# A two-layer encoder trunk on one core: page stores on other queues, one group in raw tiles, and row scaling spread over three products

## The chip, the core and the metric

The kernel runs on one core of a Trainium2 chip. A core has TensorE (PE in the profile) for matmuls, VectorE (DVE), ScalarE (ACT), GpSimd (POOL) and SyncE (SP), and 16 DMA engines that move data between HBM and the on-chip memory. Each engine works through its own list of instructions in order; semaphores tie the lists together. SP, ACT and POOL can issue DMAs; an engine whose next instruction is a DMA that may not start yet waits there, and all that follows in its list waits too. The metric is the device time of one execution in microseconds (us), as a median of several.

## The reference, cut to what matters

Two layers, each with a mixer and a SwiGLU feed-forward block, each followed by a layer norm over the residual sum. Layer 0 mixes by latent attention plus a two-dimensional Fourier transform, layer 1 by a gated unit with a 128 x 128 mixing of positions.

```python
def even_mixer(x, ...):
    h = x @ w_in
    c_q, c_kv, k_r, f = jnp.split(h, ...)
    q = (rms_norm(c_q, q_norm) @ w_uq)...   # nope part, rotary part
    k_nope, v = (c_kv @ w_uk)..., (c_kv @ w_uv)...
    attn = mla_attention(q_nope, q_rope, k_nope, k_rope, v)
    return jnp.concatenate([attn, fourier_mix(f)], axis=-1) @ w_out

def odd_mixer(x, ...):
    u, v = jnp.split(gelu(x @ w_in), 2, axis=-1)
    s = (einsum('gpq,bnqgc->bnpgc', w_s, layer_norm(v)) + b_s)
    return (u * s) @ w_out

for layer in range(2):
    y = even_mixer(x) if layer == 0 else odd_mixer(x)
    x = layer_norm(ALPHA * x + y, mix_ln_g[layer], mix_ln_b[layer])
    x = layer_norm(ALPHA * x + swiglu(x), ffn_ln_g[layer], ffn_ln_b[layer])
```

There are 1024 positions of width 1024, 8 heads, a feed-forward width of 2816, all in float32.

## The kernel before

**Numbers.** A float32 product is made of three matmuls. `split` (L133) turns an operand into a high part (ACT copies it into the matmul's rounded type, L135) and a low part (DVE subtracts, L136); `mm3` (L138) runs high x high (L141), high x low (L142) and low x high (L143). So each operand that comes from memory passes ACT, then DVE, then PE.

**Stages.** In the order of time: `even_front` (projection, norms, Fourier part) to about 150 us, `attention` to 560, the output product of the even mixer to 670, the first feed-forward block to 1330, the gated unit's front to 1680, its output product to 1840, and the second feed-forward block to the end. Between stages, data goes through pages in HBM: `mix0` to `mix11` hold the columns of the even mixer (0 to 7 the heads' outputs, 8 to 11 the Fourier groups), `tp` those of the odd mixer, `h` those of the feed-forward blocks.

**`reduce`** (L409) is the product that ends a mixer or a feed-forward block, together with the residual sum and the layer norm. It computes a 2 x 2 block product with seven products p = 1 to 7 in place of eight, which needs sums of blocks: SA, SB of the left pages, TA, TB of the weights. The sums are made ahead by `job` (L330: POOL loads two pages, DVE adds them at L317 to L320, POOL stores them). A product runs over M pairs of pages (M is 6 for the even mixer, "mix", 8 for the odd one, "odd", and 11 for the feed-forward blocks), taken two pairs at a time in n groups (3, 4 and 6). The products come in the order 1, 5, 6, 4, 7, 2, 3. Per group `load` (L440) has SP fetch the two operand tiles, one for the left side and one for the right (L396), and splits them into one of three pairs of cells (`xoh`, `xol`); PE then runs 4 position tiles x 2 pairs x 3 = 24 matmuls. The fetched tiles are called `rx`; there are six of them, placed where the stage before had its tiles. For the first two groups of "mix" `lead` (L405) fetches into raw weight tiles (`raw`, handed out in turn by `raw_tile`, L151) while attention still runs.

PE accumulates in eight banks: p = 1 uses four, p = 5 the other four; p = 6 goes on in those of p = 1, and p = 4 takes those of p = 5 over. So the sums of p = 1 must be added to the rows (`add`, L455, on DVE) before p = 6 starts, and those of p = 5 before p = 4 starts.

**Rows.** The residual rows are eight tiles, four of half 0 (`xt[0, s]`) and four of half 1. `residual` (L461) clears a word of the tile on DVE (L465), to order the tile's reuse, and POOL fetches the row block, 512 KB (L466). Except in "mix", `gained` (L468) multiplies it by the scale of the preceding layer norm and adds its bias (L472 and L473, 1024 wide, on DVE). The first `add` to a tile multiplies it by ALPHA as well (L458).

**Queues.** In the first layer SP issues, besides the weight loads (L158) and the swaps of the rotary part (L1103 and L1287), the stores of finished pages: 20 stores of the Fourier part (L1238, L1242, L1243) and 32 stores of attention's pages (L1360), each behind the ACT copy of the page (L1358). Each store waits on SP until its page is computed. The order of each engine's list is settled when the program is built; `behind` (L306) keeps an instruction behind a named one.

Of the kernel before, what the change touches and what calls it, by code (L numbers as in the profile page):

```python
# [112 lines left out]
class Trunk:  # L113
# [295 lines left out]
    def reduce(self, st, resid, rgb, ln, keep, pre=None, left=()):  # L409


        nc, a = self.nc, self.a
        lo, hi = self.LO, self.HI
        left = list(left)
        M = len(st["W"]) // 2
        groups = self.groups(st)
# [23 lines left out]
        def load(p, g):  # L440
            if (p, g) not in ops:
                with self.behind(*((self.last_a, self.last_v) if p == 1 and self.last_a is not None else ())):
                    ops[p, g] = self.stream(st, p, groups[g], raws, pairs)

        def mm(p, g, s):
            if p in (6, 7):
# [76 lines left out]


        def spread(jobs, k, of):
            i0, i1 = len(jobs) * k // of, len(jobs) * (k + 1) // of
            for j in jobs[i0:i1]:
                j()
        slots = range(4)
        for p in (1, 5, 6, 4, 7, 2):  # L530
            for g in range(n):
                load(p, g)
                if p == 1 and g == 1:
                    load(1, 2)
                    if rgb is not None:
                        rg, rb = (self.bcast(tmp(), a["ln_" + x][rgb[0], rgb[1]]) for x in "gb")
                    last = self.job(st, M - 1, True) if st is self.stage["mix"] else None
                if p == 1 and 0 < g < 3:
                    for s in (2 * g - 2, 2 * g - 1):
                        residual(0, s)  # L540
                if (p == 1 and g == n - 1) or (p == 5 and g == 0):
                    for s in (0, 1) if p == 1 else (2, 3):
                        residual(1, s)
                if p == 6 and g == 0 and keep is None:
                    fg, fb = (self.bcast(self.raw_tile(), a["ln_" + x][ln[0], ln[1]]) for x in "gb")
                if p == 4 and g == 0 and pre is not None:
                    with self.behind(*self.marks):
                        pre()
                if p == 1 and g > 1:
                    spread([lambda s=s: gained(0, s) for s in slots], g - 2, n - 1)  # L550
                if p == 5 and g == 0:
                    spread([lambda s=s: gained(0, s) for s in slots], n - 2, n - 1)
                if p == 5 and g > 0:
                    spread([lambda s=s: gained(1, s) for s in slots], g - 1, n - 1)
                if (p, g) == (5, 1):
                    for s in slots:
                        add(0, s, lo, 1, True)
                if p == 2:
                    spread([lambda s=s: normed1(s) for s in slots], g, n)
                for s in slots:  # L560
                    mm(p, g, s)
                    if p == 1 and s % 2 == 1 and left:
                        left.pop(0)()
                    if g == n - 1:
                        if p == 5:
                            add(0, s, hi, p, True)
                            add(1, s, hi, p, True)
                        elif p == 6:
                            add(0, s, hi, p)
                        elif p == 4:  # L570
                            add(1, s, lo, p, True, ALU.subtract)
                        elif p == 7:
                            add(1, s, lo, p)
                            add(1, s, hi, p)
                        elif p == 2:
                            add(0, s, lo, p)
                            stat(0, s, 0)
                if (p, g) == (5, 0) and last is not None:
                    last(self.marks[2])
# [566 lines left out]
    def fourier(self, fe, fo, f512, chan, mix):  # L1146
# [4 lines left out]
        with ExitStack() as es:  # L1151
# [75 lines left out]
            for i in range(2):  # L1227
                for j in range(2):
# [6 lines left out]
                    y, yv = y.rearrange("p (b h c) -> p b h c", b=2, h=2), ym.rearrange("p (b h c) -> p b h c", b=2, h=2)  # L1235
                    if j == 0:
                        for b in range(2):
                            nc.sync.dma_start(page[:, b], y[:, b])  # L1238
                    else:
                        for x in range(2):  # L1240
                            for b in range(2):
                                nc.sync.dma_start(page[x * H + 1:(x + 1) * H, b], y[x * H + 1:(x + 1) * H, b])  # L1242
                                nc.sync.dma_start(page[x * H:x * H + 1, b], yv[2 * i + x:2 * i + x + 1, b])  # L1243

    def attention(self, cq, ckv, kr, rc, rs, mix):
        nc, a = self.nc, self.a
        with ExitStack() as es:
# [102 lines left out]
            def pv(hp, h, qb):  # L1350
                d = st[hp]
                page, pt = T([P, 256], F32, "page"), d.pop(("ptr", h, qb))
                ps = self.mm_bank((P, 256))
                vh, vl = d["v"][h]
                for kt in range(NT):
                    ph, pl = (t[:, kt % 4, :] for t in pt[kt // 4])
                    self.mm3(ps, (vh[:, kt, :], vl[:, kt, :]), (ph, pl), kt == 0, kt == NT - 1)
                nc.scalar.copy(page, ps)  # L1358
                o = qb % 2 * 512 + qb // 2 * 256
                nc.sync.dma_start(mix[hp * 2 + h][:, o:o + 256], page)  # L1360

            def front(hp):
                qks = [lambda tb=tb, w=w: qk(hp, 0, w, tb) for w in "qk" for tb in range(2)]
# [54 lines left out]
```

## Time and profile before

| quantity | us |
|---|---|
| median of 3 runs (2510.45 to 2514.87) | 2513.96 |
| profiled execution, its own time | 2514.32 |
| its span, first to last instruction | 2512.5 |
| PE busy and idle in 150 to 560 (attention) | 401.58, 8.42 |
| PE busy and idle in 560 to 670 ("mix" reduce) | 102.69, 7.31 |
| PE busy and idle in 1185 to 1330 (ffn reduce, first) | 144.06, 0.94 |
| PE busy and idle in 1680 to 1840 ("odd" reduce) | 145.13, 14.87 |
| PE busy and idle in 2275 to 2512.5 (ffn reduce, last) | 218.44, 19.06 |

The stretches come from the view that sums each engine's busy time by windows. A row of the timeline reads: start, duration, engine, line, operation, output<-inputs, count, and in brackets the idle time ahead of it with what released it. SPq is a DMA issue on SP; its duration is the time that SP spent on it, waits of an aggregated row included. A matmul's row is longer than its step, since matmuls overlap in the pipeline.

### The profile page before, as it was taken

How to read it: one execution, taken by the hardware profiler on the slowest of the kernel's cores; microseconds unless marked ns; L12 is line 12 of the kernel's file. 1: busy time of each engine (PE TensorE's matmuls, PEld its weight loads, DVE VectorE, ACT ScalarE, POOL GpSimd, SP SyncE). 2: the span in 40 equal slices, each digit the busy share in tenths (PEclk: the TensorE clock that was granted, in tenths of full speed). 3: DMA queues.
4: the chain of work that ended last, by engine and by line, in shares of the span. 5: the costliest groups of instructions: out<-in, count | busy, mean ns of one | idle time of the engine just before them, and what ended most of it. 6: DMA issues, size and time to landing. Idle time of an engine off the chain costs nothing.

```text
span 2512.5 us, 33168 instructions
## 1 busy us (share of the span) xinstructions
PE 2446.8 (97%) x12294; PEld 2066.2 (82%) x12294; DVE 1809.2 (72%) x2569; ACT 1111.2 (44%) x1711; POOL 317.2 (13%) x527
## 2 busy tenths in 40 slices
PE   8989999998999999999999999998999999999997
PEld 6778888887888888888889998876878888887885
DVE  4348887776986776668678776868778676667767
ACT  4235555553563333334455446662464333333431
POOL 1001011000111111110002132430011111111001
PEclk9999999999999999999999999998999999999999
DMA  5132334128435444468655554577624544539654
GB/s 177 43 90 70 114 112 134 59 85 311 165 125 178 175 163 156 177 236 299 219 175 179 199 206 139 195 243 276 207 102 160 184 157 157 186 146 330 216 191 143
DMA packets 164329, 431.95 MB, mean 172 GB/s; under 512 B 20136, under 2 KB 26952, under 8 KB 164168
## 3 DMA queue, kind: packets, MB, share of 16 engines
q1 hardware_dynamic: 108216, 232.11, 28.0%
q0 software_dynamic: 55952, 197.73, 21.1%
q8 instruction: 96, 1.57, 0.3%
q14 instruction: 65, 0.53, 0.1%
HBM read 286.64 MB, written 138.41 MB: 169 GB/s over the span
## 4 chain that ended last, share of the span: by engine, by line
PE 85%; issue 5%; DVE 4%; DMA 2%; ACT 2%; SPq 1%; POOL 0%; DVEq 0%; POOLq 0%; ACTq 0%
PE b L142 19%; PE b L143 19%; PE b L141 19%; PE S L1325 6%; PE b L921 6%; PE mm L141 4%; PE mm L142 4%; PE mm L143 4%; PE mm L1344 2%; DVE xol L136 1%; PE b L857 1%; DMA rx<-w_down 1%; ACT q L378 0%; DMA gb<-ln_b 0%; ACT xoh L135 0%
## 5 line engine op out<-in xcount | busy, mean ns | idle before, releaser
L135 ACT CAST whi<-raw 128x1024 fp32r<-128x1024 f32 (+3 forms) x277 | 260.6, 951 | 385.3 <-PE b L142 223.2
L136 DVE TENSOR_TENSOR wlo<-raw,whi 128x1024 fp32r<-128x1024 f32 (+3 forms) x277 | 303.3, 1098 | 162.8 <-ACT whi L135 159.6
L135 ACT CAST xoh<-rx 128x1024 fp32r<-128x1024 f32 (+1 forms) x252 | 244.9, 1011 | 386.9 <-PE b L142 282.4
L141 PE MATMUL b<-xoh,whi 128*128 128x512 f32 x1040 | 408.0, 392 | 1.1 <-ACT xoh L135 1.0
L142 PE MATMUL b<-xol,whi 128*128 128x512 f32 x1040 | 405.1, 389 | 0.9 <-DVE xol L136 0.9
L143 PE MATMUL b<-xoh,wlo 128*128 128x512 f32 x1040 | 404.6, 389 | 0.0
L142 PE MATMUL b<-xol,xoh 128*128 128x512 f32 x960 | 378.6, 394 | 17.7 <-DVE xol L136 16.6
L136 DVE TENSOR_TENSOR xol<-rx,xoh 128x1024 fp32r<-128x1024 f32 (+1 forms) x252 | 287.2, 1167 | 144.0 <-ACT xoh L135 140.6
L141 PE MATMUL b<-xoh 128*128 128x512 f32 x960 | 372.2, 393 | 7.2 <-ACT xoh L135 7.2
L143 PE MATMUL b<-xoh,xol 128*128 128x512 f32 x960 | 376.2, 392 | 0.0
L142 PEld LDWEIGHTS b<-xol,xoh 128*128 128x128 f32 x960 | 182.4, 190 | 58.9 <-DVE xol L136 19.6
L141 PEld LDWEIGHTS b<-xoh,whi 128*128 128x128 f32 x1040 | 195.3, 188 | 42.2 <-ACT xoh L135 2.0
L142 PEld LDWEIGHTS b<-xol,whi 128*128 128x128 f32 x1040 | 195.3, 188 | 41.4 <-DVE xol L136 1.5
L143 PEld LDWEIGHTS b<-xoh,wlo 128*128 128x128 f32 x1040 | 195.2, 188 | 40.5
L141 PEld LDWEIGHTS b<-xoh 128*128 128x128 f32 x960 | 181.4, 189 | 46.2 <-ACT xoh L135 8.7
L143 PEld LDWEIGHTS b<-xoh,xol 128*128 128x128 f32 x960 | 182.4, 190 | 37.9
L672 ACT COPY y<-b 128x512 f32<-128x512 f32 x200 | 116.5, 585 | 187.1 <-PE b L143 179.7
L141 PE MATMUL b<-xah,whi 128*128 128x512 f32 x416 | 162.5, 391 | 0.8 <-ACT xah L135 0.8
L142 PE MATMUL b<-xal,whi 128*128 128x512 f32 x416 | 162.0, 389 | 0.0
L143 PE MATMUL b<-xah,wlo 128*128 128x512 f32 x416 | 161.9, 389 | 0.0
L131 DVE TENSOR_TENSOR raw<-raw,raw 128x512 f32<-128x512 f32 (+1 forms) x174 | 128.3, 738 | 27.0 <-DMA raw<-w_up 23.5
L717 DVE TENSOR_TENSOR y<-b,y 128x512 f32<-128x512 f32 x84 | 57.9, 689 | 74.7 <-PE b L143 74.5
(381 smaller groups left out, 4587.3 us busy)
## 6 DMA issues: line engine op xcount, KB each, us to landing
raw<-w_gate SPq DMA_DIRECT2D x44, 512.0 KB, 3.7
raw<-w_up SPq DMA_DIRECT2D x44, 512.0 KB
q<-w_down POOLq DMA_DIRECT2D x44, 512.0 KB, 5.3
h<-x POOLq DMA_DIRECT2D x44, 512.0 KB, 4.1
rx<-h SPq DMA_DIRECT2D x60, 256.0 KB, 3.2
rx<-w_down SPq DMA_DIRECT2D x60, 256.0 KB, 4.2
raw<-o_v SPq DMA_DIRECT2D x16, 512.0 KB, 4.7
x<-o_out POOLq DMA_DIRECT2D x16, 512.0 KB, 6.1
```

The costliest lines, as they stand in the source:

```text
L131: self.nc.vector.tensor_tensor(out, a, b, op=ALU.subtract)
L135: a = self.nc.scalar.copy(hi, src)
L136: return a.ins, self.nc.vector.tensor_tensor(lo, src, hi.bitcast(F32), op=ALU.subtract).ins
L141: mm(ps, lh, rh, start=start, stop=False, skip_group_check=skip)
L142: mm(ps, lh, rl, start=False, stop=False, skip_group_check=skip)
L143: mm(ps, ll, rh, start=False, stop=stop, skip_group_check=skip)
L672: nc.scalar.copy(t, ps)
L717: self.last_v = nc.vector.tensor_tensor(sb, ps, sb, op=op).ins
L857: nc.tensor.matmul(ss[:, s, :], vt[:, s, :], wsT[:, g, :], start=True, stop=True)
L921: nc.tensor.matmul(ps[:, i * 256:(i + 1) * 256], l[:, b, k, c], r[:, k, :], start=start and k == 0 and i == 0 and m == 0, stop=k == 3 and ...
L1325: nc.tensor.matmul(sc[:, kb, :], l[:, s], r[:, kb * 512:(kb + 1) * 512], start=i == 0, stop=i == 4)
L1344: nc.tensor.transpose(ps[:, k, :], p[:, kt * P:(kt + 1) * P], self.ident)
```

## The change

In `reduce`:

- The loads of the residual rows of half 1 move from the last group of p = 1 and group 0 of p = 5 to groups 0 and 1 of p = 5.
- `gained` of half 0 was spread over the groups from p = 1, g = 2 to p = 5, g = 0; now the first tile is done at the last group of p = 1 and the other three over p = 5. `gained` of half 1 was spread over p = 5; now the first tile is done at its last group and three over p = 6.
- The sums of p = 1 into half 0 were added at (5, 1), all four together; now they are spread over the groups of p = 5 from g = 1 on.
- The sums of p = 5 were added to both halves at the end of p = 5, eight adds; now those of half 1 are spread over the groups of p = 6 from g = 1 on.
- In "mix" the third group of p = 1 is fetched into two raw tiles in place of two `rx` tiles.

In the first layer the 20 stores of the Fourier part are issued by POOL and the 32 of attention by ACT, right behind the copy that fills the page.

```diff
-                    ops[p, g] = self.stream(st, p, groups[g], raws, pairs)
+                    ops[p, g] = self.stream(st, p, groups[g], self.raw_tile if st is self.stage["mix"] and (p, g) == (1, 2) else raws, pairs)
...
-            i0, i1 = len(jobs) * k // of, len(jobs) * (k + 1) // of
+            i0, i1 = (min(len(jobs), len(jobs) * i // of) for i in (k, k + 1))
...
-                if (p == 1 and g == n - 1) or (p == 5 and g == 0):
-                    for s in (0, 1) if p == 1 else (2, 3):
+                if p == 5 and g in (0, 1):
+                    for s in (0, 1) if g == 0 else (2, 3):
                         residual(1, s)
...
-                if p == 1 and g > 1:
-                    spread([lambda s=s: gained(0, s) for s in slots], g - 2, n - 1)
-                if p == 5 and g == 0:
-                    spread([lambda s=s: gained(0, s) for s in slots], n - 2, n - 1)
-                if p == 5 and g > 0:
-                    spread([lambda s=s: gained(1, s) for s in slots], g - 1, n - 1)
-                if (p, g) == (5, 1):
-                    for s in slots:
-                        add(0, s, lo, 1, True)
+                if p == 1 and g == n - 1:
+                    gained(0, 0)
+                if p == 5:
+                    spread([lambda s=s: gained(0, s) for s in (1, 2, 3)], g, n - 1)
+                    if g > 0:
+                        spread([lambda s=s: add(0, s, lo, 1, True) for s in slots], g - 1, n - 1)
+                    if g == n - 1:
+                        gained(1, 0)
+                if p == 6:
+                    spread([lambda s=s: gained(1, s) for s in (1, 2, 3)], g, n - 1)
+                    if g > 0:
+                        spread([lambda s=s: add(1, s, hi, 5, True) for s in slots], g - 1, n - 1)
...
                         if p == 5:
                             add(0, s, hi, p, True)
-                            add(1, s, hi, p, True)
...
-                            nc.sync.dma_start(page[:, b], y[:, b])
+                            nc.gpsimd.dma_start(page[:, b], y[:, b])
...
-                                nc.sync.dma_start(page[x * H + 1:(x + 1) * H, b], y[x * H + 1:(x + 1) * H, b])
-                                nc.sync.dma_start(page[x * H:x * H + 1, b], yv[2 * i + x:2 * i + x + 1, b])
+                                nc.gpsimd.dma_start(page[x * H + 1:(x + 1) * H, b], y[x * H + 1:(x + 1) * H, b])
+                                nc.gpsimd.dma_start(page[x * H:x * H + 1, b], yv[2 * i + x:2 * i + x + 1, b])
...
-                nc.sync.dma_start(mix[hp * 2 + h][:, o:o + 256], page)
+                nc.scalar.dma_start(mix[hp * 2 + h][:, o:o + 256], page)
```

Three places show how the lists change. First SP's list at the start of attention; `yT` and `ym` are Fourier pages, `w_uqn` and `w_ukv` weights of the second pair of heads, `rw<-rt` the swaps of the rotary part. Before:

```order
L1242 DMA mix_88<-yT_1407 126x1x256 x2
L1243 DMA mix_88<-ym_1379 2x1x256
L158 DMA raw_1987<-w_uqn 128x768
L1103 DMA rw_1462<-rt_1461 32x512 x4
L158 DMA raw_1993<-w_ukv 128x1024
```

and now:

```order
L158 DMA raw_1981<-w_uqr 128x384
L158 DMA raw_1987<-w_uqn 128x768
L158 DMA raw_1993<-w_ukv 128x1024
L1105 DMA rw_1462<-rt_1461 32x512 x4
L1289 DMA qs_1449<-rw_1462 64x512
```

Of the Fourier stores the last three are shown. Those between `w_uqr` and `w_uqn` are gone from SP, and `w_ukv` now stands ahead of the swaps. On ACT the cast of `w_uqn` stood behind the copy of `rt` and two casts of `qh`; it now stands ahead of them.

Second, SP's list at the end of attention; `mix_81` and `mix_83` are the pages mix4 and mix6 of the third group, `mix_84` is mix7. Before:

```order
L1360 DMA mix_84<-page_5315 128x256
L1360 DMA mix_84<-page_5445 128x256
L1360 DMA mix_84<-page_5523 128x256
L1360 DMA mix_84<-page_5565 128x256
L396 DMA rx_5654<-mix_81 128x512
L396 DMA rx_5654<-mix_83 128x512
L396 DMA rx_5659<-w_out 128x512 x2
L396 DMA rx_5728<-mixSB_119 128x512
```

and now:

```order
L396 DMA raw_5364<-w_out 128x512 x2
L396 DMA raw_5654<-mix_81 128x512
L396 DMA raw_5654<-mix_83 128x512
L396 DMA raw_5659<-w_out 128x512 x2
L396 DMA rx_5724<-mixSB_119 128x512
```

The first row is the end of the second group's load; that of the third follows on it, into raw tiles, with no page store between. Further down, the load of the last sum (mixSB_5) and the matmuls of (5, 2), which use it, stand behind (6, 0) before and ahead of (6, 0) now.

Third, DVE's list in the "odd" reduce, behind the last split of p = 1; `x` with `gb` are L472 and L473, L317 to L320 the last sum of pages, `xol<-rx` the low part of an operand; the two that are shown belong to (5, 0). Before:

```order
L472 TENSOR_TENSOR x_14844<-x_14844,gb_14926 128x1024
L465 MEMSET x_14840 128x1
L465 MEMSET x_14841 128x1
L473 TENSOR_TENSOR x_14844<-x_14844,gb_14928 128x1024
L317 TENSOR_TENSOR x_14640<-x_14639,x_14640 128x512
L472 TENSOR_TENSOR q_14845<-q_14845,gb_14926 128x1024
L318 TENSOR_TENSOR x_14639<-x_14639 128x512
L473 TENSOR_TENSOR q_14845<-q_14845,gb_14928 128x1024
L319 TENSOR_TENSOR x_14639<-x_14640,x_14639 128x512
L136 TENSOR_TENSOR xol<-rx_15042,xoh 128x1024
L320 TENSOR_TENSOR x_14640<-x_14640,x_14639 128x512
L136 TENSOR_TENSOR xol<-rx_15047,xoh 128x1024
```

and now:

```order
L472 TENSOR_TENSOR x_14844<-x_14844,gb_14926 128x1024
L136 TENSOR_TENSOR xol<-rx_15036,xoh 128x1024
L317 TENSOR_TENSOR x_14640<-x_14639,x_14640 128x512
L473 TENSOR_TENSOR x_14844<-x_14844,gb_14928 128x1024
L318 TENSOR_TENSOR x_14639<-x_14639 128x512
L136 TENSOR_TENSOR xol<-rx_15041,xoh 128x1024
L319 TENSOR_TENSOR x_14639<-x_14640,x_14639 128x512
L465 MEMSET x_14840 128x1
L465 MEMSET x_14841 128x1
L320 TENSOR_TENSOR x_14640<-x_14640,x_14639 128x512
L472 TENSOR_TENSOR q_14845<-q_14845,gb_14926 128x1024
```

Ahead of the second split of (5, 0) stood four wide operations and four narrow ones; now two of each.

## Prediction

> **What bounds the kernel now.** I read the page first: busy shares and the chain that ended last.
>
> ```profile
> PE 2446.8 (97%) x12294; PEld 2066.2 (82%) x12294; DVE 1809.2 (72%) x2569; ACT 1111.2 (44%) x1711; POOL 317.2 (13%) x527
> PE 85%; issue 5%; DVE 4%; DMA 2%; ACT 2%; SPq 1%; POOL 0%; DVEq 0%; POOLq 0%; ACTq 0%
> ```
>
> TensorE is busy 2446.8 of 2512.5 us and holds 85% of the chain. No matmul is removed, so the change can only win TensorE's idle time, 2512.5 − 2446.8 = 65.7 us, and time at a lowered clock. The second view is therefore the timeline of PE, for rows with idle time ahead of them, and for each releaser the view of waits.
>
> ```profile
> PE b L142 <- DVE xol L136: 17.5, 10, 4.9
> 178.50 0.58 PE L141 MATMUL mm<-whi,ckv0h 128*128 128x256 f32 x1 [6.87 <-DVE kl L136]
> 588.47 0.50 PE L141 MATMUL b<-xoh 128*128 128x512 f32 x1 [2.37 <-ACT xoh L135]
> 589.73 0.76 PE L142 MATMUL b<-xol,xoh 128*128 128x512 f32 x1 [0.76 <-DVE xol L136]
> 599.61 0.50 PE L141 MATMUL b<-xoh 128*128 128x512 f32 x1 [3.91 <-ACT xoh L135]
> 1711.51 0.80 PE L142 MATMUL b<-xol,xoh 128*128 128x512 f32 x1 [4.93 <-DVE xol L136]
> 1726.05 1.19 PE L141 MATMUL b<-xoh 128*128 128x512 f32 x4 [0.95 <-ACT xoh L135]
> 1741.95 0.80 PE L142 MATMUL b<-xol,xoh 128*128 128x512 f32 x1 [4.72 <-DVE xol L136]
> ```
>
> Three places hold the waits that the change can touch: the start of attention (6.87), the mix reduce (2.37 + 0.76 + 3.91 = 7.04) and the odd reduce (4.93 + 0.95 + 4.72 = 10.60). The third view is a table by stretches; its last three columns are the granted clock, DMA share and GB/s.
>
> ```profile
> 178.50:190.00 11.50, 11.50 (x57) 10.58 (x58) 7.46 (x14) 5.30 (x12) 1.25 (x1) 0.78 0.35 92
> 200.00:550.00 350.00, 349.64 (x2199) 309.61 (x2198) 280.38 (x433) 184.82 (x350) 34.21 (x51) 1.00 0.30 98
> 570.00:600.00 30.00, 22.96 (x93) 17.98 (x92) 16.16 (x20) 9.71 (x10) 4.91 (x10) 0.94 1.04 406
> 589.73:595.70 5.97, 5.97 (x18) 4.46 (x18) 1.98 (x2) 2.10 (x2) 0.00 (x0) 0.71 1.04 402
> 599.61:606.00 6.39, 6.39 (x21) 5.14 (x22) 3.41 (x5) 0.00 (x0) 0.00 (x0) 0.73 0.63 232
> 1711.51:1726.00 14.49, 13.58 (x49) 10.74 (x49) 14.04 (x17) 4.00 (x4) 1.07 (x2) 0.84 0.77 258
> 1741.95:1750.00 8.05, 8.05 (x25) 6.45 (x26) 4.49 (x5) 1.09 (x2) 0.00 (x0) 0.69 0.94 291
> ```
>
> Behind each of these waits PE works at a lowered clock: (1 − 0.78) × 11.5 = 2.5 us are lost at the first place, 1.7 + 1.7 = 3.4 in mix, 2.3 + 2.5 = 4.8 in the odd reduce. In 200:550, without waits, the clock is 1.00. So what can be had is 6.87 + 2.5 = **9.4**, 7.04 + 3.4 = **10.4** and 10.60 + 4.8 = **15.4** us. At 589.73 the clock is low after 2.37 and 0.76 together, so a rest of some 3 us can cost 1.7 to 2.5 more.
>
> **Start of attention.**
>
> ```profile
> 157.33 0.63 SPq L1238 DMA_DIRECT2D mix<-yT  x1
> 170.65 0.35 SPq L158 DMA_DIRECT2D raw<-w_uqn  x1
> 171.11 2.49 SPq L1103 DMA_DIRECT2D rw<-rt  x4
> 174.99 0.83 ACT L135 CAST whi<-raw 128x768 fp32r<-128x768 f32 x1 [6.88 <-DMA raw<-w_uqn]
> 161.40 0.59 ACT L1101 COPY rt<-mm 128x512 f32<-128x512 f32 x1 [2.31 <-PE mm L143]
> 161.13 0.55 DVE L136 TENSOR_TENSOR wlo<-raw,whi 128x384 fp32r<-128x384 f32 x1
> 175.77 1.26 POOL L1110 TENSOR_TENSOR rw<-rw,rope_s 128x512 f32<-128x512 f32 x1 [18.00 <-DMA rw<-rt]
> 179.57 0.68 DVE L1111 TENSOR_TENSOR rt<-rt,rw 128x512 f32<-128x512 f32 x1
> 185.83 0.40 PE L1325 MATMUL S<-krh,qs 128*128 128x512 f32 x1
> ```
>
> From 157.33 to 170.65 SyncE issues Fourier stores; only then comes w_uqn, and its cast blocks ACT until 174.99, ahead of the kh casts that PE waits for. With these stores on POOL's queue the load follows the DVE row that frees its slot, 161.13 + 0.55 = 161.7; with the same 4.3 from issue to cast (174.99 − 170.65) it is there at 166.0. The cast now stands ahead of the rt copy and the q casts on ACT; ACT is idle there, and rt is ready near 166.0 + 0.83 + 0.59 = 167.4 instead of 162.0; PE works through its other banks meanwhile, with no rest that I can bound by a row, so I allow it up to 1. The low part, twice the 0.55 of half its width, ends near 166.9 + 1.1 = 168, frees w_ukv's load on SP, and the four swaps behind it issue from 168.3 to 170.8. POOL's multiply came 2.2 us after the swaps' end (175.77 − 173.60), so now 173.0 to 174.2; POOL's own stores, sixteen in this time at the 0.54 of POOL's row at 579.53 (below), are 8.6 us from 157.3 on and end before that. L1111 then runs at 174.3 instead of 179.57, and S<-krh follows by at most its old distance of 185.83 − 179.57 = 6.26, at 180.6: a gain of 5.3. If PE's own work is the limit it comes 9.4 earlier. Some of the old distance was PE at a lowered clock, so I take **7**; 4 if a rest lowers the clock again.
>
> **Page stores on ACT.**
>
> ```profile
> L135 ACT CAST pth<-mm 128x512 fp32r<-128x512 f32 x121 | 69.6, 589 | 46.9 <-PE mm L1344 40.3 <-PE mm L143 4.4 <-ACT qh L135 0.2
> L1358 ACT COPY page<-mm 128x256 f32<-128x256 f32 x30 | 11.2, 372 | 13.8 <-PE mm L143 13.7
> ```
>
> No DMA issued by ACT is in this trace. The bounds come from SP's rows: 0.35 for a load and 0.63 for a store above, times 32, so 0 (all hidden) to 20 (all stores on the path). In 200:550 ACT is busy 184.8 of 350 us and waits for PE both ahead of the 30 page copies (13.7 in all) and ahead of the probability casts (40.3), which stand behind a store on ACT and which PE waits for in its turn. So I stand near hidden. Behind the last pages nothing more comes to hide it: I take a **loss of 1**, two stores at 0.5, and 4 as an end.
>
> **Mix reduce.**
>
> ```profile
> 547.23 12.44 SPq L1360 DMA_DIRECT2D mix<-page  x3
> 559.77 0.88 SPq L396 DMA_DIRECT2D rx<-mix  x2
> 563.88 1.05 ACT L135 CAST xoh<-rx 128x1024 fp32r<-128x1024 f32 x1 [4.56 <-DMA rx<-mix]
> 579.53 0.54 POOL L341 DMA_DIRECT2D mixSB<-raw  x1 [0.66 <-DVE raw L320]
> 593.37 0.32 SPq L396 DMA_DIRECT2D rx<-mixSB  x1
> 598.51 1.04 ACT L135 CAST xoh<-rx 128x1024 fp32r<-128x1024 f32 x1 [3.60 <-DMA rx<-mixSB]
> ```
>
> SP stands at the last page until 559.67; then all loads start at once and the DMA engines are full (1.04, 406 GB/s in 570:600). The load of the last sum, mixSB_5, goes out at 593.37, and its cast at 598.51 releases the 3.91 wait. Now SP holds no page; the third group, 1 MB, goes into raw tiles freed earlier and half of the first SB tile, 0.5 MB, can go too: 1.5 MB / 406 GB/s = 3.7 us less for the crowded stretch. The third group's cast no longer waits for 563.88 but runs when the pages end, by 559.7: memsets, residual loads and last sums, which stand behind it on DVE, come about 4 us sooner; 2 MB of residuals of half 1 move back by a group. Against it: by the new order (5,2), which needs mixSB_5, stands before (6,0), so PE wants it at 588.47 − 2.37 = 586.1 instead of 599.61 − 3.91 = 595.7. Its store was issued at 579.53, its load only at 593.37, because SP stood in front of full rx tiles. Four us sooner is 575.5; add 3 to 5 for the store to land and 5.1 from load to cast (598.51 − 593.37), and 1.05 + 1.2 for the split: ready at 586 to 588, later by what SP still waits for tiles. With a rest of 1 to 4 us I take a gain of **7**, ends 3 and 10.4. If the cover is gone, the wait of 7 comes back at one place.
>
> **Odd reduce.**
>
> ```profile
> 1701.50 1.23 DVE L472 TENSOR_TENSOR x<-x,gb 128x1024 f32<-128x1024 f32 x1 [4.92 <-DMA x<-xs]
> 1704.42 0.69 DVE L317 TENSOR_TENSOR x<-x,x 128x512 f32<-128x512 f32 x1 [0.43 <-DMA tp<-x]
> 1710.24 1.22 DVE L136 TENSOR_TENSOR xol<-rx,xoh 128x1024 fp32r<-128x1024 f32 x1
> 1734.75 1.28 DVE L458 SCALAR_TENSOR_TENSOR x<-x,b 128x512 f32<-128x512 f32 x2
> 1739.54 6.90 DVE L136 TENSOR_TENSOR xol<-rx,xoh 128x1024 fp32r<-128x1024 f32 x6
> ```
>
> ```profile
> 1691.00 0.39 PE L142 MATMUL b<-xol,xoh 128*128 128x512 f32 x1
> ...
> 1694.41 0.39 PE L142 MATMUL b<-xol,xoh 128*128 128x512 f32 x1
> ```
>
> DVE works in program order. Before the second xol of group (5,0) stood four scale and bias operations and four sums, so it ran at 1710.24 and PE at 1711.51. Now two of the wide operations and two sums stand there. L472 still waits for its load until 1701.5 and L317 until 1704.42; a wide operation takes 6.90 / 6 = 1.15 start to start, a 512-wide one (1739.54 − 1734.75) / 8 = 0.6. From 1704.42 on, L317, L473, L318 and xol end at 1704.42 + 0.6 + 1.15 + 0.6 + 1.22 = 1708.0, where PE is free at 1711.51 − 4.93 = 1706.6: a rest of 1.4. The second wait was eight adds in a row, 1734.75 to 1739.54; four of them now go between the products of p = 6. As a check I count DVE from 1701.5 through p = 5 and p = 6: 16 xol and 16 wide operations, 12 adds and 4 sums, in all 32 × 1.15 + 16 × 0.6 = 46.4, so the last xol, two adds from the end, is ready near 1701.5 + 46.4 − 1.2 + 0.6 (L317's wait) = 1747.3. PE takes 24 matmuls a group at 3.41 / 15 = 0.227 (15 steps from 1691.00 to 1694.41), 5.46; it wants the eighth group at 1706.6 + 7 × 5.46 = 1744.8. The rests sum to 2.5 or 3, none long. Gain 15.4 − 2.9 = **12.5**; ends 8 (rests of 5 and a lowered clock) and 15.4.
>
> **The ffn reduces** have the same rearranged adds. The xol row has 17.5 − 4.93 − 4.72 − 0.76 = 7.1 left over seven waits, most of them where nothing moves: **0.5**, ends −1 and 3. That raw tiles change places in the ffn has no wait to meet in these views: 0.
>
> **Sum.** 7 − 1 + 7 + 12.5 + 0.5 = 26. The profiled execution took 2514.32 against a median of 2513.96, so it stands for the runs: 2514.3 − 26 = **2488**.
>
> **Rivals.** First, mix stays bound by DMA: the traffic is the same, share 1.04, and (5,2) is wanted earlier, so the wait only changes its place. Then 7 are missing: 2495. For it: 406 GB/s; against: the engines are at a low share until 560, and 1.5 MB go there.
>
> Second, the moved queues bring nothing, since the transfers meet the same sixteen engines whoever issues them. Then only 12.5 + 0.5 − 1 remain: 2502. Against it: in 178.5:190 the DMA share is 0.35 and the first row behind 170.65 that waits is ACT's for w_uqn, so SP's order and not the engines held w_uqn. The Trainium skill (DMA: Bandwidth & Descriptors, "Issuing engines are not separate DMA queues") says that DMAs of all issuers interleave on the same engines, and that several issuers save only sequencer time, usually little; by that rule 2502 would be the likelier. The trace agrees on the sharing in 570:600, but the 13.3 us of SP between 157.33 and 170.65 are sequencer time and waits.
>
> Third, DVE becomes the bound of the odd reduce: per group 2 × 1.15 for xol, 2 × 1.15 for scale and bias and one or two adds of 0.6, 5.2 to 5.8 against PE's 5.46. If semaphores and loads add 0.7 a group over seven groups, 5 us are lost and, with the clock, 3.4 more: 2488 + 8.4 = 2496.
>
> Fourth, slower: the ACT queue. A store waits on ACT for its own copy and holds the probability casts behind it. It decides from 27 / 32 = 0.84 us a store on the path; at 1.1 us each the loss is 35 instead of 1, and the time 2488 − 1 + 35 = 2522. Against it: ACT's idle time. For it: the attention has no idle PE, so every delay beyond the slack of one block shows.
>
> **How the numbers follow.** Forecast 0.62; mix bound by DMA 0.13; queues bring nothing 0.09; DVE bound 0.08; ACT slower 0.04; 0.04 for a mixture that ends near no change. Ends of the forecast: all won is 9.4 + 10.4 + 15.4 + 3 = 38, 2476; the low ends give 4 + 3 + 8 − 1 − 4 = 10, 2504. The range 2477 to 2504 takes in the first three rivals. Within 0.2% (5 us, about what a measurement of this kernel can tell from no change) lie 2509 to 2519: 0.04; faster 0.92; slower 0.04.
>
> **What would show it.** Right: after about 160 SP issues w_uqn by 162 and PE's 6.87 row is gone or under 3; SP's page rows in 520 to 560 are gone; the waits near 588, 599, 1711 and 1742 are each under 2.5 and the clock there 1.00; PE in 200:550 still idles under 2. Wrong: rows of PE waiting for pth or ptl in the attention; a wait at (5,2) for mixSB of 4 us or more; xol late in every group of p = 5 and 6.

## The result

The changed kernel takes 2491.38 us (median of 4 runs, 2490.29 to 2494.98) against 2513.36 us of the kernel before (2510.45 to 2514.87): a ratio of 0.9917, with an interval of 0.9902 to 0.9933, 22 us. The forecast was 2488 in a range of 2477 to 2504. The sum came out near, 22 won for 26 forecast, but three of its terms came out smaller, and a term that it didn't have makes up for much of what they lack.

The page of the changed kernel, busy shares and the chain that ended last:

```profile
PE 2442.8 (98%) x12294; PEld 2063.7 (83%) x12294; DVE 1809.5 (73%) x2569; ACT 1112.4 (45%) x1711; POOL 330.9 (13%) x547
PE 87%; issue 5%; DVE 4%; ACT 2%; DMA 2%; POOL 1%; SPq 0%; DVEq 0%; ACTq 0%; POOLq 0%
```

PE's idle time fell from 65.7 to 2489.0 − 2442.8 = 46.2 us, and DVE's and ACT's work is the same. The timeline of PE, rows with idle time ahead of them, at the places that the prediction named (lines up to L540 keep their numbers, those behind the changed part of `reduce` are two higher):

```profile
176.37 0.39 PE L141 MATMUL mm<-whi,ckv0h 128*128 128x256 f32 x1 [3.33 <-DVE kl L136]
587.52 0.80 PE L141 MATMUL b<-xoh 128*128 128x512 f32 x1 [5.47 <-ACT xoh L135]
1680.73 0.91 PE L859 MATMUL b<-q,wlo 128*128 128x128 f32 x6 [3.48 <-ACT xoh L135]
1715.77 0.50 PE L142 MATMUL b<-xol,xoh 128*128 128x512 f32 x1 [2.14 <-DVE xol L136]
```

The start of attention went from 6.87 to 3.33, the mix reduce from 7.04 in three waits to 5.47 in one, the odd reduce from 10.60 in three to 2.14 in one. The third row has grown: ahead of the odd reduce's products PE waits 3.48, where before it waited 2.24:

```profile
1686.10 0.35 PE L857 MATMUL b<-q,wlo 128*128 128x128 f32 x1 [2.24 <-ACT xoh L135]
```

The view by stretches, behind each wait (the last columns: granted clock, DMA share, GB/s):

```profile
200.00:550.00 350.00, 349.79 (x2212) 310.36 (x2211) 281.27 (x434) 186.63 (x352) 33.76 (x51) 1.00 0.31 103
176.37:188.00 11.63, 11.10 (x53) 9.24 (x54) 8.03 (x14) 5.84 (x13) 1.76 (x2) 0.85 0.19 47
587.52:606.00 18.48, 18.44 (x68) 14.54 (x69) 14.36 (x17) 6.81 (x7) 0.00 (x0) 0.84 0.76 258
1680.73:1700.00 19.27, 17.65 (x70) 14.09 (x71) 14.42 (x20) 6.39 (x7) 4.38 (x9) 0.82 0.96 345
1715.77:1730.00 14.23, 14.23 (x56) 11.57 (x57) 14.23 (x16) 7.75 (x8) 0.00 (x0) 0.88 0.75 254
```

PE idles 0.21 in 200:550, so the stores on ACT cost nothing that can be seen there. But the lowered clock is still behind each of the four waits: 0.15 x 11.63 = 1.7, 0.16 x 18.48 = 3.0, 0.18 x 19.27 = 3.5 and 0.12 x 14.23 = 1.7 us. The third is an upper bound: PE waits another 1.61 us while the clock is low, and works 5.19 of the 6.80 us at half clock, which makes 2.6:

```profile
1682.20:1689.00 6.80, 5.19 (x14) 3.60 (x13) 6.80 (x11) 1.16 (x2) 2.07 (x4) 0.50 0.95 307
```

To weigh the stages apart, I took from each trace the starts of the same matmul by its number in PE's list: 500 to 800 (start of attention), 800 to 2400 (attention), 2800 to 3300 (mix reduce), 8000 to 9300 (odd reduce and what leads to it), and the end of the span behind PE's last matmul. The labels are those of the experiments below.

| kernel | start | attention | mix | odd | end | median us |
|---|---|---|---|---|---|---|
| before | 63.5 | 260.8 | 100.8 | 289.6 | 16.0 | 2513.4 |
| e1_before_again | 63.2 | 260.8 | 100.8 | 289.2 | 16.0 | 2513.1 |
| changed | 59.7 | 260.4 | 98.6 | 280.3 | 11.2 | 2491.4 |
| e2_queues_only | 59.4 | 261.1 | 97.3 | 289.7 | 11.2 | 2500.8 |
| e3_rows_only | 63.1 | 261.0 | 101.7 | 278.8 | 15.7 | 2502.2 |
| e4_third_in_rx | 58.3 | 260.6 | 99.4 | 281.1 | 11.2 | 2492.7 |
| e5_swaps_first | 56.8 | 261.5 | 99.2 | 279.6 | 11.2 | 2487.7 |
| e6_page_halves | 59.6 | 261.2 | 100.1 | 279.7 | 11.2 | 2494.4 |
| e7_sums_by_act | 60.8 | 261.0 | 97.6 | 278.9 | 11.1 | 2490.9 |
| e8_rows_late | 61.1 | 261.2 | 96.9 | 281.3 | 11.2 | 2491.4 |
| e9_longer_list | 63.5 | 261.4 | 102.6 | 288.0 | 15.7 | 2511.6 |
| e10_pages_only | 63.6 | 261.1 | 99.3 | 289.9 | 16.0 | 2509.4 |
| e11_both_late | 57.3 | 261.3 | 97.9 | 280.6 | 11.2 | 2490.7 |
| e12_stores_twice | 73.0 | 261.3 | 100.6 | 288.2 | 11.0 | 2512.6 |

From before to changed: 3.8 at the start, 0.4 in attention, 2.2 in mix, 9.4 in odd, 4.8 at the end; 0.8 more between matmuls 9300 and 9600, and 2.5 in the last ffn reduce, of which e1 shows 2.0 without any change; 3300 to 8000 is 0.5 longer.

How far these numbers can be read is seen where the code is the same. The start is 58.3 to 61.1 in changed, e2, e4, e6, e7 and e8; mix is 100.6 to 102.6 in before, e1, e9 and e12, and 98.6 to 100.1 in changed, e5 and e6. The runs were made on several chips, on which the kernel before took 2510.8 to 2513.4; each ratio below is against the kernel before on the same chip.

### The profile page after: what moved, and what is told of

Its sections match the earlier page's. It is cut to its first block, busy times and chain, and to the rows that moved or that the text cites. A ratio compares the mean times of both kernels' runs of the same rounds, so it can differ in the third digit from the quotient of the medians.

```text
span 2489.0 us, 33155 instructions
## 1 busy us (share of the span) xinstructions
PE 2442.8 (98%) x12294; PEld 2063.7 (83%) x12294; DVE 1809.5 (73%) x2569; ACT 1112.4 (45%) x1711; POOL 330.9 (13%) x547
## 3 DMA queue, kind: packets, MB, share of 16 engines
q0 software_dynamic: 57168, 199.84, 21.6%
## 4 chain that ended last, share of the span: by engine, by line
PE 87%; issue 5%; DVE 4%; ACT 2%; DMA 2%; POOL 1%; SPq 0%; DVEq 0%; ACTq 0%; POOLq 0%
PE b L142 20%; PE b L143 20%; PE b L141 20%; PE S L1327 6%; PE b L923 6%; PE mm L141 4%; PE mm L142 4%; PE mm L143 4%; PE mm L1346 2%; PE b L859 1%; DVE xol L136 1%; DMA y<-x 0%; ACT q L378 0%; DMA tp<-x 0%; ACT x L378 0%
```

## Experiments

**The kernel before again (e1).** No edit.

> The kernel before, unchanged, as a measure of what repeats. Theory A (the waits inside the program repeat, the landing of the last store does not): PE's waits of 6.87, 2.37 + 0.76 + 3.91, 4.93 and 4.72 come again within 0.3 us, while the time from PE's last matmul to the end of the span, 16.0 us in the first profile of before and 11.2 in that of the change, comes out anywhere between 11 and 16. Theory B (the change itself shortens the end by 4.8 us): the end is 16 us again. Time 2510 to 2515 by both.

PE's waits came as 6.39, 1.75 + 0.77 + 4.09, 3.85 and 4.56 with the stretches of the table. Three of the waits (6.39, 1.75 and 3.85) differ by more than the 0.3 expected, but the stages of the table agree to 0.4. The end is 16.0 to a hundredth: theory A falls, the 4.8 us are the change's. The two waits of the last ffn reduce (0.76 and 1.08) are absent here, so most of its 2.5 us is scatter between executions.

**Only the stores (e2), only the rows (e3).** e2 is the kernel before with the lines of the diff that change the issuer; e3 is the changed kernel with these undone and `raws` in place of the raw tile.

```diff
-                nc.sync.dma_start(mix[hp * 2 + h][:, o:o + 256], page)
+                nc.scalar.dma_start(mix[hp * 2 + h][:, o:o + 256], page)
...
-                            nc.sync.dma_start(page[:, b], y[:, b])
+                            nc.gpsimd.dma_start(page[:, b], y[:, b])
```

> Only the stores move (Fourier pages to POOL, attention's pages to ACT); rows, adds and the third group as before. Theory A (SP's order held the loads): the wait of 6.87 at the start of attention falls to about 3.3 as in the changed kernel, the loads of the mix reduce start by 556 instead of 560, the waits of 4.93 and 4.72 in the odd reduce stay; 4 to 8 us faster, 2505 to 2509. Theory B (all queues end on the same engines, moving issuers brings nothing): the wait of 6.87 stays within 1 us, time 2512 to 2515. Theory C (stores on ACT cost on attention's path): PE idles over 5 us in 200 to 550 and the time is 2515 or more.

> Only the rows, scales and adds of reduce change; all stores on SP and the third group in rx tiles as before. Theory A (the odd and ffn gains come from DVE's order alone): the waits of 4.93, 0.95 and 4.72 in the odd reduce become one or two under 2.5, those of the last ffn reduce (0.76, 1.08) go, the 6.87 at the start stays; 11 to 14 us faster, about 2501, if the mix reduce stays as it was. Theory B (the gains need the earlier loads too): under 6 us faster.

e2 is 2500.8 (ratio 0.9955, 0.9938 to 0.9971), faster than theory A expected; e3 is 2502.2 (0.9956, 0.9941 to 0.9971), just under theory A's 11 to 14. The two halves, 12.0 and 10.7, add up to the whole. In e2 the start falls to 59.4 with a wait of 3.01; the odd reduce stays, with waits of 2.63 and 4.83 for 4.93 and 4.72. In e3 the odd reduce falls to 278.8 and the rest stays, with mix at 101.7 inside the scatter of the kernel before. Of e2's 12 us, 4.0 are the start, 3.5 mix and 4.8 the end. So the gain in mix comes with the stores. PE's rows of e3 in the odd reduce are:

```profile
1686.99 1.62 PE L859 MATMUL b<-q,wlo 128*128 128x128 f32 x6 [2.09 <-ACT xoh L135]
1691.07 0.50 PE L142 MATMUL b<-xol,xoh 128*128 128x512 f32 x1 [0.44 <-DVE xol L136]
1708.52 0.50 PE L142 MATMUL b<-xol,xoh 128*128 128x512 f32 x1 [1.52 <-DVE xol L136]
```

The first rest at (5, 0) is 1.52, where 1.4 was forecast. And the wait ahead of the products is 2.09 here, as before: that it grows to 3.48 comes with the stores, not with the rows.

**The third group in rx (e4).**

```diff
-                    ops[p, g] = self.stream(st, p, groups[g], self.raw_tile if st is self.stage["mix"] and (p, g) == (1, 2) else raws, pairs)
+                    ops[p, g] = self.stream(st, p, groups[g], raws, pairs)
```

> The changed kernel with the third group of the mix reduce fetched into rx tiles again. Theory A (early fetch of that group is what the mix reduce gains): PE waits for it near 556 to 560 or for later groups, 3 to 7 us slower than the changed kernel, 2494 to 2498. Theory B (the mix reduce is bound by the last sum, mixSB_5, whose store waits 10.9 us to land among the other transfers): the wait at (5, 2) is again 4 to 6 us and nothing else appears; within 2 us of the changed kernel.

2492.7 us, mix 99.4 against 98.6, waits of 2.23, 0.66 and 2.58, in sum 5.47, the same to a hundredth. Kernels in which this stage is the same by the code differ by as much (changed 98.6, e5 99.2, e6 100.1), so no gain from the raw tiles is shown. Theory B's time came out, though the wait has three places and not one.

**What holds the start of attention (e5).** Rows of the changed kernel, of SP, ACT and DVE:

```profile
161.67 0.33 SPq L158 DMA_DIRECT2D raw<-w_uqn  x1
165.67 0.84 ACT L135 CAST whi<-raw 128x768 fp32r<-128x768 f32 x1 [6.43 <-DMA raw<-w_uqn]
167.53 0.33 SPq L158 DMA_DIRECT2D raw<-w_ukv  x1
167.95 2.85 SPq L1105 DMA_DIRECT2D rw<-rt  x4
175.02 0.69 DVE L1111 TENSOR_TENSOR rt<-rt,rope_c 128x512 f32<-128x512 f32 x1 [4.86 <-DMA rw<-rt]
175.63 0.68 DVE L136 TENSOR_TENSOR kl<-mm,kh 128x512 fp32r<-128x512 f32 x1
```

The swaps end their issue at 170.80 and are through only at 175.0, 4.2 us later. They read `rt`, which the next operation of DVE overwrites, so DVE waits for them; the second low part of the keys (`kl`), for which PE waits, stands behind that operation. e5 loads w_ukv of the second pair of heads behind the swaps. (The lines that set `self.swap` are left out.)

```diff
-                st[hp] = {"ur": self.unit(a["w_uqr"][hp], 3), "un": self.unit(a["w_uqn"][hp], 3), "ukv": self.unit(a["w_ukv"][hp], 2)}
+                st[hp] = {"ur": self.unit(a["w_uqr"][hp], 3), "un": self.unit(a["w_uqn"][hp], 3)}
+                with self.behind(self.swap if hp == 1 else None):
+                    st[hp]["ukv"] = self.unit(a["w_ukv"][hp], 2)
```

> The changed kernel with w_ukv of the second pair of heads loaded behind the first four swaps instead of ahead of them; nothing else. In the changed kernel the swaps are issued from 167.95 to 170.80 and read only at 175.0, and the low part of the keys waits behind that on DVE (PE's wait of 3.33). Theory A (the 512 KB of w_ukv, issued right ahead, hold the swaps up on the DMA engines): the swaps land within 3 us of their issue, PE's waits at 172 to 181 sum to under 1.5, and the stretch from the Fourier part to the attention is 2 to 5 us shorter; about 2488. Theory B (the Fourier stores issued by POOL, which run on the same engines until about 170, hold them): the waits stay at 2.5 to 4 us, time as the changed kernel.

```profile
165.81 2.99 SPq L1105 DMA_DIRECT2D rw<-rt  x4
170.79 0.69 DVE L1111 TENSOR_TENSOR rt<-rt,rope_c 128x512 f32<-128x512 f32 x1 [1.93 <-DMA rw<-rt]
172.13 0.38 PE L141 MATMUL mm<-whi,ckv0h 128*128 128x256 f32 x1 [0.40 <-DVE kl L136]
176.03 0.36 PE L141 MATMUL mm<-whi,ckv0h 128*128 128x256 f32 x1 [1.75 <-DVE vl L136]
```

The swaps are through 2.0 us behind their issue (168.80 to 170.79), the wait of 3.33 is 0.40, and a wait of 1.75 for `vl` is next. The stretch is 2.9 shorter, the median 2487.7 (0.9906, 0.9891 to 0.9921), the fastest of all here. Theory A came out but for the sum of the waits, 2.15 where under 1.5 was expected. Between these two profiles, 512 KB right ahead of four swaps of 64 KB cost them 2.2 us. Over all kernels with the stores on POOL it is less even: in the six with w_ukv ahead, DVE gets past the swaps 1.9 (e4) to 4.2 us behind their issue and the start takes 58.3 to 61.1; with it behind (e5, e11) these are 2.0 and 1.7, and 56.8 and 57.3. The Fourier stores are in the same crowd: in each of these eight traces the last of them lands 0.4 to 0.8 us ahead of the last swap, at 174.29 in the changed kernel and at 170.23 in e5. What they cost alone no run shows.

**What ACT pays for a store (e6).** Each page is stored in two halves, 64 stores in place of 32.

```diff
-                nc.scalar.dma_start(mix[hp * 2 + h][:, o:o + 256], page)
+                for b in range(0, 256, 128):
+                    nc.scalar.dma_start(mix[hp * 2 + h][:, o + b:o + b + 128], page[:, b:b + 128])
```

> The changed kernel with each of the 32 page stores of attention issued by ACT as two stores of half the size, so ACT issues 64. Theory A (stores on ACT lie in its idle time): PE's idle time in 200 to 550 stays under 1 us and the time within 2 us of the changed kernel. Theory B (each is on the path): 32 x 0.33 = 10.6 us slower than the changed kernel, about 2502.

The rows by source line give the price of one issue in the changed kernel:

```profile
L1362 ACTq DMA_DIRECT2D mix<-page x32: 326/326/345, 206.7 to 555.3; - x32
```

One issue takes 0.33 us, and twice as many are not 10.6 us more: attention takes 261.2, within what kernels with 32 stores take (260.4 to 261.5). The last stores do show: a wait for `pth` of 0.57 at 551 in the changed kernel is 1.05 here, and the stretch from matmul 2400 to 2800 goes from 62.0 to 62.7. The median, 2494.4 (0.9937, 0.9917 to 0.9956; four runs from 2491.6 to 2500.7), lies 3.0 above that of the changed kernel, where theory A allowed 2, but the intervals overlap. By the stretches it is theory A.

**What holds mixSB_5 (e7, e8).** In the changed kernel the load of this sum is issued at 581.41, because its store, issued by POOL at 570.51, took 10.9 us to land, while the DMA engines were full (the view by stretches, first row, has a DMA share of 1.03):

```profile
570.00:582.00 12.00, 12.00 (x54) 9.64 (x52) 6.29 (x8) 3.06 (x3) 3.00 (x6) 1.00 1.03 414
570.51 0.54 POOL L341 DMA_DIRECT2D mixSB<-raw  x1 [0.19 <-issue]
581.41 0.32 SPq L396 DMA_DIRECT2D rx<-mixSB  x1
586.42 1.05 ACT L135 CAST xoh<-rx 128x1024 fp32r<-128x1024 f32 x1 [8.00 <-DMA rx<-mixSB]
```

e7 stores the last two sums from ACT's queue; e8 fetches the residual rows of half 1 later.

```diff
-                nc.gpsimd.dma_start(st[d][m], r)
+                (nc.scalar if st is self.stage["mix"] and m == 5 and pages else nc.gpsimd).dma_start(st[d][m], r)
...
+                if p == 5 and rgb is None and g == n - 1:
+                    for s in slots:
+                        residual(1, s)
+                if p == 5 and rgb is not None and g in (0, 1):
```

> The changed kernel with the two sums of the last job of the mix reduce (mixSA_5, mixSB_5) stored by ACT instead of POOL. Theory A (their stores stand in POOL's queue behind the residual rows that POOL fetches): mixSB_5 lands within 6 us of its issue instead of 10.9, the wait at (5, 2) falls from 5.47 to under 2.5; 3 to 6 us faster than the changed kernel, about 2487. Theory B (all DMA engines are full there, whichever queue): landing stays at 8 to 11 us and the wait at 4 to 6.

> The changed kernel with the four residual rows of half 1 of the mix reduce (2 MB, of which 1 MB is issued ahead of the last sums' stores) fetched at the last group of p = 5 instead of its groups 0 and 1. Theory A (the crowded stretch is bound by the bytes ahead of mixSB_5): its store lands 2.5 us or more sooner and the wait at (5, 2) falls to 2 to 3.5; 2 to 5 us faster. Theory B (order on SP's list holds the load, not bytes): the wait stays at 5 to 6; time as the changed kernel. Theory C: the rows are then missing at p = 6, with a new wait of 2 us or more near 595 to 605.

The last line of the view by tile for mixSB, of the kernel before, of e7 and of e8; the longest is the sum in question:

```profile
DMA to landing us min/median/max: 2.9/4.3/13.8
```

```profile
DMA to landing us min/median/max: 2.6/3.9/10.1
```

```profile
DMA to landing us min/median/max: 2.6/3.8/7.3
```

In e7 the store, from a queue with only the other sum ahead of it, still took 10.1 us and PE waited 5.31: theory B, the engines are full (DMA share 1.03 in 570:582) whichever queue. In e8, with 1 MB less ahead, it landed 3.6 us sooner and its load went out at 580.07, but that load, now among the late rows, took 6.6 us to its cast in place of 5.0, so PE still waited 4.41, and there is no new wait at p = 6. That is 1.1 us less than in the changed kernel, but less than kernels with the same stage differ by (5.47, 5.74 in e5, 6.82 in e6), and in e11, which has this edit too, the store lands after 7.1 us and PE waits 5.72. So the bytes ahead of the store set much of the time that it takes to land; that the stage becomes shorter with fewer of them is not shown. Medians 2490.9 and 2491.4, as the changed kernel.

**The end of the span (e9, e12) and pages alone (e10).** The rows by source line for the last line of the program show what differs at the end, the instruction DRAIN on POOL (before, then changed; the three durations are shortest, middle and longest, in ns, then come the first and the last start):

```profile
L1414 POOLq DRAIN  x3: 46/93/9527, 2501.9 to 2512.0; - x3
L1414 SPq DRAIN  x3: 7/7/7, 2506.7 to 2511.7; - x3
```

```profile
L1416 POOLq DRAIN  x3: 46/102/3327, 2483.2 to 2488.8; - x3
L1416 SPq DRAIN  x3: 7/7/7, 2488.2 to 2488.5; - x3
```

Before, SP reaches its DRAINs at 2506.7 and its last one starts only at 2511.7, behind POOL's, which ends at 2501.95 + 9.53 = 2511.5: POOL sets the end. In the changed kernel POOL's ends at 2483.22 + 3.33 = 2486.5 and SP, which issues the last stores, gets to its DRAINs at 2488.2: now SP sets the end. So of the 6.2 us by which POOL's DRAIN is shorter, 4.8 show. e9 lengthens POOL's list without moving a store; e10 moves the attention pages alone; e12 keeps the Fourier stores on SP and has POOL issue each again, into spare pages that nothing reads.

```diff
+            for _ in range(20):
+                nc.gpsimd.memset(few, 0.0)
...
                             nc.sync.dma_start(page[:, b], y[:, b])
+                            nc.gpsimd.dma_start(spare[:, b], y[:, b])
```

> The kernel before with 20 memsets of one column added to POOL's list early, at about the place where the change adds 20 stores; no store moves. Theory A (how long POOL's list is decides where POOL itself stalls: the end of the span behind PE's last matmul, 16.0 before and 11.2 with the stores on POOL, and PE's wait near 1677 to 1684 of 2.2 before and 3.5 with them): the end becomes 11.2 and the wait 3.4 or more, without any store moved; 1 to 5 us faster than before. Theory B (the stores' queue does it, since SP has less to finish at the end): the end stays 16.0 and the wait 2.2; 2510 to 2515.

> The kernel before with only attention's 32 page stores moved to ACT. Theory A (each move acts at its own place): the wait of 6.87 at the start of attention stays, the mix reduce takes 97 to 98 us in place of 100.8 between the same two matmuls, the end stays 16.0 and the wait near 1684 at 2.2, because POOL's list is as before; 3 to 4 us faster, about 2509. Theory B (the mix reduce gains from the start of attention or POOL's list): it stays at 100 or more, time within 1.5 us of before.

> The kernel before, with each of the 20 Fourier stores left on SP and issued a second time by POOL into four spare pages that nothing reads. Theory A (what ends the span sooner is something that POOL's added DMAs leave behind, as the number of its instructions is not it): the end behind PE's last matmul is 11.2 instead of 16.0 and the wait near 1684 is 3.4 or more, although SP still has its stores; the wait of 6.87 at the start of attention stays or grows. Theory B (SP, relieved of its stores, ends sooner): the end stays 16.0 and the wait 2.2. Time 2508 to 2514 by A, 2512 to 2518 by B.

e9: 2511.6, a ratio of 0.9997 (0.9987 to 1.0006), the end 15.7, the wait ahead of the odd products 1.87: theory A falls, the number of POOL's instructions is not it. e10: 2509.4 (0.9987, 0.9977 to 0.9997), start, end and odd wait (2.28) as before, mix 99.3, so theory A in kind, with 1.5 of the 3 us expected in mix. e12, 2512.6 (0.9998, 0.9988 to 1.0008):

```profile
L1418 POOLq DRAIN  x3: 46/102/3327, 2507.1 to 2512.4; - x3
1696.64 1.52 PE L858 MATMUL b<-q,wlo 128*128 128x128 f32 x6 [3.31 <-ACT xoh L135]
```

Theory A: with POOL's 20 added stores the DRAIN is 3.33 and the odd wait 3.31, although SP still has its own. So both come with the DMAs that POOL issues in addition, and neither from SP's relief. What it gains at the end it loses at the start, 73.0 in place of 63.5: with 2 MB more of stores SP issues w_uqn at 180.17 instead of 170.65, and PE waits 10.28 for `kl`.

**Two edits together (e11).** e5's and e8's.

> The changed kernel with both edits that shortened a stretch: w_ukv behind the swaps (start of attention 56.8 in place of 59.7) and the residual rows of half 1 of the mix reduce fetched late (96.9 in place of 98.6). Theory A (they add): 4 to 5 us faster than the changed kernel, about 2486. Theory B (the second only moves waits to later groups): as with the first alone, 2487.7, within 0.7 us.

2490.7 (0.9913, 0.9899 to 0.9928): start 57.3 and mix 97.9 are both shorter than in the changed kernel, by 2.4 and 0.7, but the median is not clear of it. By the ratios e5 alone stays the best, with overlapping intervals. Neither theory's time came out. In the profiles e11 is longer than e5 in stretches that its edits don't touch (2.3 us ahead of matmul 500, 1.0 in odd); over all fourteen kernels the time ahead of matmul 500 is 124.4 to 127.7, so that part is scatter.

## Why the prediction was right, step by step

- **Bound.** Right: PE's busy time is 2442.8 of 2489.0 us, and all that was won is idle time, the end included, and lowered clock.
- **Start, 7 forecast, 3.8 came.** The step that failed is "POOL's multiply came 2.2 us after the swaps' end, so now 173.0 to 174.2". SP's part was right to 0.4 us (w_uqn at 161.67, its cast at 165.67, the swaps from 167.95), but by the new order w_ukv's 512 KB run just ahead of the swaps, and these were through 4.2 us behind their issue in place of 2.0; e5 shows it by moving that one load. The path was also another: the prediction leads from the swaps over POOL's multiply to `S<-krh`, but PE waits for `kl`, which on DVE stands behind the operation that waits for the swaps. That the lowered clock might come back (the end of 4) is what happened, 1.7 us.
- **Stores on ACT, −1 forecast, nothing measurable came.** e6 bounds it: 32 more stores cost some 0.7 us at the end of attention.
- **Mix, 7 forecast, 2.2 came.** The first rival, that the stage stays bound by DMA and the wait only changes its place, is what happened, nearly in full. The step that failed is "add 3 to 5 for the store to land": it took 10.9, while the engines were full. The trace of before could have told. There the same store took 13.8 us, from 579.53 to 593.4, and its load went out at 593.37, as it landed; the prediction put that delay down to full rx tiles. That the store went out 9.0 us sooner, where 4 were forecast, kept the loss down. The Trainium skill (DMA: Bandwidth & Descriptors, "Issuing engines are not separate DMA queues") says that DMAs interleave on the same engines whoever issues them; e7 agrees, 10.1 us from a queue with one other store ahead. Its other half, that several issuers save only a little sequencer time, the trace doesn't bear out: e2 moves nothing but issuers and gains 4.0 us at the start and 3.5 in mix, since SP stood in order at stores that were not ready.
- **Odd, 12.5 forecast, 9.4 came.** The products' waits fell by 8.5 (10.60 to 2.14), 0.8 more than forecast, and the count of DVE's operations gave the first rest to 0.1 in e3. The term that failed is the lowered clock: 4.8 us were to be won, but 1.7 are still lost behind the wait of 2.14, and 2.6 ahead of the products, behind the wait that went from 2.24 to 3.48, which no step of the prediction has. e12 shows that it comes with POOL's stores. In e3, with 2.09 there and one lowering of the clock in place of two, the stretch gains 10.3 against e1.
- **ffn, 0.5 forecast.** The profile has 2.5, but e1 has 2.0 of them too: nothing is shown.
- **The end, not forecast, 4.8 came.** No step asked what lies behind PE's last matmul; it was POOL's DRAIN.
- **Its own signs.** w_uqn by 162, no page rows on SP and PE's idle time under 2 in 200:550 came. The first wait was to be under 3 and is 3.33, the clock was to be 1.00 and is not, and a sign of being wrong came, the wait at (5, 2) of 4 us or more.

The terms that repeat sum to 3.8 + 0.4 + 2.2 + 9.4 + 0.8 + 4.8 = 21.4; the medians differ by 22.0. Without the end the time would be near 2496, in the range still, as the first rival had it: the forecast took too much from the two places where DMA decides, and a term that nobody had asked for filled the gap. That the time came within 4 us of 2488 is in this part luck; the order of SP's list, DVE's count and the price of stores on ACT were right by their reasons.

## What to carry to other kernels

Where an engine's list holds a transfer behind stores that are not ready, moving those stores to an engine that has the data in hand can win as much as the load is late, but then look at what runs first on the DMA engines: here a large load just ahead of small, urgent transfers went with a start of 58.3 to 61.1 us, and behind them of 56.8 and 57.3. In a stage at a DMA share of 1 the better order of queues gave 2.2 of 7 us forecast. Take the time that a transfer needs to land there from that stage of the trace before (13.8 us here), and not from a quiet one. Spread long helper work between the operands that PE waits for, and count the helper engine's total against PE's, since both counts here came out within a microsecond. And look at what ends the span behind the last matmul.

## What was not expected of the hardware

- POOL's DRAIN at the end is 9.53 us in the kernel before and in e9, with 55952 packets on POOL's queue, and 3.33 in the changed kernel and e12, with 57168; in e7, with 56880, it is 2.76. In the table the end is 15.7 to 16.0 in all five kernels without the added stores and 11.0 to 11.2 in all nine with them. Which property of the number decides stays open.
- With the same stores, an issue of POOL comes later some 1500 us after them:

```profile
1670.38 0.72 POOL L838 DMA_DIRECT2D wlo<-vd  x1 [1.46 <-PE b L859]
```

  In the kernel before, this load of `wlo` is issued right behind the one ahead of it. Whether the matmul named is the cause is not shown, since the order there is the same in both. In e7, with two POOL stores fewer, PE's wait there is 2.09 again, and one of 2.19 stands ahead of 1514.33. The cause stays open.
- Whether a wait lowers the clock depends on where it falls. The traces record each change of the granted clock: it is 1.00 or 0.50 (other values in the views are means), and within a trace the changes lie whole multiples of 3.41 us apart. Counted in such steps, from 20 us to PE's last matmul in all fourteen traces, PE idles 1.80 us or more in 60 of the 10002 steps at 1.00, and 57 of these are followed by a step at 0.50; of the other 9942 steps one is. In the kernel before, waits of 2.24 and 2.02 near 1686 are cut by the borders of the steps, so that none holds more than 3.41 − 1.74 = 1.67 us of idle time, and the clock stays at 1.00:

```profile
1682.12:1685.53 3.41, 1.74 (x12) 1.42 (x10) 2.27 (x4) 3.41 (x6) 0.00 (x0) 1.00 0.94 368
1685.53:1688.94 3.41, 2.06 (x12) 1.57 (x12) 3.41 (x6) 2.44 (x4) 1.62 (x3) 1.00 0.86 336
1688.94:1692.36 3.42, 2.17 (x9) 1.80 (x10) 3.42 (x5) 0.53 (x1) 0.55 (x1) 1.00 1.00 308
1692.36:1695.77 3.41, 3.41 (x16) 2.82 (x15) 3.41 (x9) 0.93 (x1) 1.11 (x3) 1.00 0.86 308
```

  In the changed kernel the single wait of 2.14 lies whole in one step, and the next is at 0.50:

```profile
1712.88:1716.29 3.41, 1.27 (x6) 0.77 (x5) 3.41 (x4) 0.11 (x1) 0.00 (x0) 1.00 1.03 406
1716.29:1719.70 3.41, 3.41 (x9) 2.64 (x9) 3.41 (x5) 3.41 (x4) 0.00 (x0) 0.50 0.96 371
```

  A step at 0.50 costs up to 1.7 us of PE's work, so some of the differences between stages hang on where the borders lie. Ahead of the odd products, 2.09 in e3, 1.87 in e9 and 2.28 in e10 lowered the clock, where 2.24 in before did not.
